# A two-layer hybrid block on one core: rotation tables from phases summed once for all groups, factors stored in three parts, scans woven two steps sooner

## The chip, the core and the metric

The kernel runs on one core of one Trainium2 chip. The metric is the device time of one execution in microseconds (us). Five engines work at once, each through its own list of instructions, in order: PE multiplies matrices (PEld is its weight load, which overlaps), DVE and ACT do element-wise work (ACT also table functions such as Sin, Silu and Gelu), POOL does a little of both, SP only issues DMAs. ACT and POOL issue DMAs too; the rows mark such issues with a q (SPq, ACTq, POOLq).

## What is computed

The reference runs two layers over 1024 latent tokens and 256 context tokens of width 1024. Layer 0 has gated linear recurrences. Layer 1, where the change lies, has windowed attention beside a bidirectional diagonal state-space model ("S5"): 64 groups of 16 channels, each with 64 complex states per direction. Cut to what matters:

```python
lam = lax.complex(lam_re[direction], lam_im[direction])
dt = jnp.exp(log_dt[direction])[:, None]
abar = jnp.exp(lam * dt)
bbar = ((abar - 1.0) / lam)[:, :, None] * bmat
st_c = diag_scan(abar, order(jnp.einsum('blgh,gph->lbgp', uc_cx, bbar)), None)
st_l = order(diag_scan(abar, order(jnp.einsum('blgh,gph->lbgp', ul_cx, bbar)), st_c[-1]))
y_l = y_l + read(st_l)        # real part of states times cmat
```

After it come a gelu, a gated linear unit (GLU) of width 2 x 1024 and the output projection.

## The kernel before, in words

Nearly all matmul work is `mm3` (lines 69 to 71): each fp32 product as three products of a high and a low part. A weight unit of 128x1024 arrives by a DMA from SP (`wraw`, L116) and is split into `whi` (ACT, L64) and `wlo` (DVE, L65).

**Layer 1** (`layer1`) weaves two generators. `main` has 88 steps, each one matmul group and its evacuation: 24 for u (S5's input, written to DRAM by L950), 10 for v, 6 for k and 48 for queries and gates; k and q go through `rope` (L895 on ACT, L897 to L899 on DVE, DMAs from ACT, L902 and L970). `side` is S5's `run`, then eight steps that read S5's output z back (`zr`, L941) and split it (`zh`, `zl`) for the GLU, whose matmuls need all of z. `weave(main, side, nm, ns)` takes a step of `side` whenever it is behind the ratio ns/nm of the steps of `main`. It fixes the order in which the program is written. The order on each engine is then laid out ahead of time by the framework's planner, from planned durations, with the earlier written instruction first where several are ready; so an engine's list does not follow the written order strictly, and once laid out it is kept.

**S5.** The states' powers are taken out of the scan: the drive is rotated by a table of cos and sin, scanned with a real decay, and rotated back. The work goes in 32 pairs of groups:
- `params` (L1290 on, once): step sizes, factors and powers for all 64 groups, on DVE, in a pool of its own ("s5t") that is given up after it. The factors lie in one tile `blk` of 128x16x512: columns 384 to 512 the powers (L1368 to L1371), 0 to 192 the outputs 0 to 2 (L1414 to L1420), 192 to 384 the outputs 3 to 5 (L1421 to L1428). One DMA of SP (L1429) writes it to DRAM when all is there. `build_a` reads 16 pieces of it back (`bq`, L1486).
- `table_a` (ACT, L1557 and L1558): r, the whole turns of n times the phase, for n = 0 to 159, of the two groups.
- `table_b` (DVE): n times the phase's high and low part, less r (L1567, L1568, each once per group), and what is left of whole turns (L1569, L1570).
- `table_c` (ACT): sin, absolute value, cos (L1579 to L1581) and the decay (`dec`, L1583).
- `front_a` (PE L1605, ACT L1609 to L1611): the drive `sd`. `front_b` (DVE L1622 to L1632): rotate, scan (L1626), rotate back into `uw`, which has two buffers; ACT copies it to `sx` (L1634, L1635). `back` (PE L1645 and L1647, ACT L1649; every fourth pair a Gelu, L1651, and DMAs of POOL, L1654).
- `build_a` and `build_b` make the matrices of four groups by turns (DVE L1545 to L1547, PE L1498 to L1521, DMAs L1526 and L1529).

After the weave `g_att` (attention) starts beside the GLU; its first loads (`kr`, L1103) go into memory that `main`'s operands held until then.

Of the kernel before, what the change touches and what calls it, by code (L numbers as in the profile page):

```python
# [9 lines left out]
F32 = mybir.dt.float32  # L10
# [3 lines left out]
AF = mybir.ActivationFunctionType  # L14
OP = mybir.AluOpType
# [39 lines left out]
class Body:  # L55
# [848 lines left out]
    def layer1(self):  # L904
# [23 lines left out]
        with tc.tile_pool(name="psum1", bufs=1, space=PSUM, reuse_waits="tile") as ps5:  # L928
            s5 = S5(self, ps5, uF, zF)
            nu = [0]  # L930
            zx = ExitStack()
            hz = []

            def side():
                yield from s5.run(nu)
                zp = zx.enter_context(tc.tile_pool(name="zt", bufs=1, reuse_waits="tile"))
                zh, zl = (zp.tile([128, 8, 1024], F32R, name=f"z{x}") for x in "hl")
                hz.extend([zh[:, :, c:c + 512], zl[:, :, c:c + 512], c, 512] for c in (0, 512))
                for cb in range(8):
                    t = zp.tile([128, 1024], F32, name="zr", tag="zr", bufs=2)  # L940
                    nc.sync.dma_start(t, zF[cb].rearrange("g h t n -> (g h) (t n)"))  # L941
                    self.split(zh[:, cb], zl[:, cb], t)
                    yield

            def main():
                for i in range(8):
                    def ev_u(ps, c0, n):
                        t = self.stg.tile([128, 512], F32, name="sg", tag="sg", bufs=2)[:, :n].rearrange("p (t n) -> p t n", t=8)
                        S.activation(t, ps.rearrange("p (n t) -> p t n", t=8), AF.Copy)
                        self.nc.scalar.dma_start(  # L950
                            uF[i * 8:i * 8 + 8, :, c0 // 8:(c0 + n) // 8].rearrange("g (h t) n -> (g h) t n", t=8), t)

                    yield from self.g_fm(st, self.hs, ev_u)
                    nu[0] += 1

                def ev_v(ps, b):
                    t = self.stg.tile([128, 512], F32, name="sg", tag="sg", bufs=2)[:, :256]
                    S.activation(t, ps, AF.Copy)
                    self.nc.scalar.dma_start(vD[b], t)

                yield from self.g_tm(st, self.hs, ev_v)
                for i in range(2):
                    def ev_k(ps, c0, n):
                        if c0:
                            self.rope(ps, c0, n, 1.0, [kD[i, o:o + 32, c0:c0 + n] for o in (0, 64, 32, 96)])
                            return
                        r = self.stg.tile([128, 512], F32, name="rp", tag="rp", bufs=3)
                        S.activation(r[:, :n], ps, AF.Copy)
                        for j, o in enumerate((0, 64, 32, 96)):
                            self.nc.scalar.dma_start(kD[i, o:o + 32, :n], r[j * 32:j * 32 + 32, :n])  # L970

                    yield from self.g_fm(st, self.hs, ev_k)
                self.h1c.close()
                for kind, i in oB:
                    def ev(ps, c0, n):
                        lc = slice(c0 - 256, c0 - 256 + n)
                        if kind == "q":
                            self.rope(ps, c0, n, 0.125, [
                                qD[lc.start // 128:lc.stop // 128, i // 2, a * 32:a * 32 + 32,
                                   i % 2 * 2 + h].rearrange("b d t -> d b t")  # L980
                                for a in range(2) for h in range(2)])
                        elif kind == "ga":
                            t = self.silu(ps, n)
                            self.nc.scalar.dma_start(gaD[i, :, lc], t)
                        else:
                            t = self.stg.tile([128, 8, 64], F32, name="sg", tag="sg", bufs=2)
                            S.activation(t, ps.rearrange("p (n t) -> p t n", t=8)[:, ::-1], AF.Silu)
                            self.nc.scalar.dma_start(gsD[i, :, :, lc.start // 8:lc.stop // 8], t)

                    yield from self.g_fm(st, self.hs[1:], ev)  # L990

            weave(main(), side(), 24 + 10 + 6 + 2 * len(oB) - 4, s5.steps + 9)
        self.right.close()
        if self.stop == "l1":
            self.show(qD, kD, vD, gaD, gsD, zF)
# [260 lines left out]
class S5:  # L1256
# [33 lines left out]
    def params(self):  # L1290
# [75 lines left out]
        for i in range(2):  # L1366
            q = pw[:, i].rearrange("p (c g) t -> p c g t", g=4)
            V.tensor_copy(pg[0:64, i], q[0:64, :, :, 7::-1])  # L1368
            V.tensor_copy(pg[64:128, i], q[64:128, :, :, 0:8])
            V.tensor_copy(pg[0:64, 2 + i], q[0:64, :, :, 8:0:-1])  # L1370
            V.tensor_copy(pg[64:128, 2 + i], q[64:128, :, :, 1:9])  # L1371
        yield

        ts(a, wr, 8.0, None, op0=OP.mult)
# [26 lines left out]
        tt(b, b, b, op=OP.mult)  # L1401
        ts(c8, b, -2.0, 1.0, op0=OP.mult, op1=OP.add)
        yield

        t1 = self.wt("s5t", (128, 16, 4, 16), 1)

# [3 lines left out]
        def out(i):  # L1410
            return blk[:, :, i * 64:i * 64 + 64].rearrange("p c (g h) -> p c g h", g=4)
# [6 lines left out]
        tt(t1, br, col(1), op=OP.mult)  # L1418
        stt(out(1), out(1), -1.0, t1, op0=OP.mult, op1=OP.subtract)
        ts(out(2), out(0), -1.0, None, op0=OP.mult)  # L1420
        tt(out(4), cr, col(5), op=OP.mult)  # L1421
        tt(t1, ci, col(6), op=OP.mult)
        tt(out(4), out(4), t1, op=OP.add)
# [2 lines left out]
        tt(t1, cr, col(6), op=OP.mult)  # L1426
        tt(out(5), out(5), t1, op=OP.subtract)
        ts(out(3), out(5), -1.0, None, op0=OP.mult)  # L1428
        self.nc.sync.dma_start(self.K.s5blk.rearrange("c p n -> p c n"), blk)  # L1429
        yield  # L1430

    def run(self, nu):
# [1 line left out]
        nc, left, tile_pool = self.nc, ExitStack(), self.K.tc.tile_pool  # L1434
        par = left.enter_context(tile_pool(name="s5p", bufs=1, reuse_waits="tile"))
        self.k5 = par.tile([128, 8, 64], F32, name="s5k5")
        self.nidx = par.tile([128, 322], F32, name="nidx")
        nc.sync.dma_start(self.nidx, self.A["nidx"])
        with tile_pool(name="s5t", bufs=1, reuse_waits="tile") as self.work:
            yield from self.params()  # L1440
# [10 lines left out]
        build()  # L1451
        yield
        build()
        self.table_a(0)
        self.table_b(0)
        self.table_c(0)
        yield
# [1 line left out]
        for p in range(32):  # L1459
            assert nu[0] * 4 > p  # L1460
            q = self.front_a(p)
            if p < 31:
                self.table_a(p + 1)
            yield
            self.front_b(q)
            if p < 31:
                self.table_b(p + 1)
            yield
            todo.append(q)
            if len(todo) > 2:  # L1470
                self.back(todo.pop(0))
            if p < 31:
                self.table_c(p + 1)
            build()
            yield
# [73 lines left out]
    def col(self, i, p, g):  # L1549
        return self.k5[:, i, p * 2 + g:p * 2 + g + 1]  # L1550

    def table_a(self, p):

        n, mag, nmag = (self.nidx[:, a:b] for a, b in ((0, 160), (320, 321), (321, 322)))
        r = self.wt("tb", (128, 2, 160), 2)
        for g in range(2):
            self.S.activation(r[:, g], n, AF.Identity, scale=self.col(7, p, g), bias=mag)  # L1557
        self.S.activation(r, r, AF.Identity, bias=nmag)  # L1558
        self.tabs[p] = r

    def table_b(self, p):

        V = self.V
        n, r = self.nidx[:, :160], self.tabs[p]
        u = self.wt("tb", (128, 2, 160), 2)
        for g in range(2):
            V.scalar_tensor_tensor(u[:, g], n, self.col(3, p, g), r[:, g], op0=OP.mult, op1=OP.subtract)  # L1567
            V.scalar_tensor_tensor(u[:, g], n, self.col(4, p, g), u[:, g], op0=OP.mult, op1=OP.add)  # L1568
        V.tensor_scalar(r, u, MAG, MAG, op0=OP.add, op1=OP.subtract)  # L1569
        V.tensor_tensor(u, u, r, op=OP.subtract)  # L1570
        self.tabs[p] = r, u

    def table_c(self, p):

        S = self.S
        w, u = self.tabs[p]
        tab = self.wt("tab", (128, 2, 2, 160), 2)
        dec = self.wt("dec", (128, 2, 2, 160), 2)
        S.activation(tab[:, :, 1], u, AF.Sin, scale=TURN)  # L1579
        S.activation(w, u, AF.Abs)  # L1580
        S.activation(tab[:, :, 0], w, AF.Sin, scale=-TURN, bias=self.K.halfpi)  # L1581
        for g in range(2):
            S.activation(dec[:, :, g], self.nidx[:, None, 160:320].to_broadcast([128, 2, 160]), AF.Copy,  # L1583
                         scale=self.col(2, p, g))
        self.tabs[p] = tab, dec

# [27 lines left out]
    def front_b(self, q):  # L1614
# [10 lines left out]
        Q = RQ[:, 0]  # L1625
        V.tensor_tensor_scan(*(x.rearrange("p a b n -> p (a b n)") for x in (Q, dec, D)), 0.0, op0=OP.mult, op1=OP.add)  # L1626
        sh = [128, 2, 2, 2, 128]
        UW = self.wt("uw", sh, 2)
        tt(UW, Q[:, :, :, None, 31:159].to_broadcast(sh), tab[:, None, :, :, 32:160].to_broadcast(sh), op=OP.mult)
        U, W = UW[:, 0], UW[:, 1]  # L1630
        tt(U[:, :, 0], U[:, :, 0], W[:, :, 1], op=OP.add)
# [54 lines left out]
def s5_host(f, A):  # L1686
# [15 lines left out]
    for h in range(16):  # L1702
        d[112 + h, :, h] = f["s5_d"][0][:, h]
    A["s5d"] = d
    A["nidx"] = np.broadcast_to(np.concatenate([np.arange(160), np.arange(160) > 0, [MAG, -MAG]]), (128, 322)).astype(np.float32)
    sh = np.zeros((128, 128), np.float32)
    sh[np.arange(16), np.arange(16) + 112] = 1
    A["shift"] = sh
# [88 lines left out]
```

## Time and profile before

| | |
|---|---|
| runs timed | 3: 2754.64, 2755.33, 2758.05 us |
| median | 2755.33 us |
| the profiled execution | 2752.66 us, span 2750.9 us |
| PE, DVE, ACT busy | 96%, 69%, 51% of the span |
| layer 1's weave and the start of the GLU | about 1565 to 2170 us of the span |

The busy times count what the profiler saw at work; PE's matmuls are pipelined, so its 96% is not a measure of how near it is to its peak. "PEclk" is the granted clock of the matrix engine as a share of 2.4 GHz; it has two levels, 1.2 and 2.4 GHz, and a stretch's number is their mean. A row of idle time names what ended most of it.

### The profile page before, as it was taken

The numbers are of one execution on the slowest core, as the hardware profiler recorded it, in microseconds if no ns is written. First come the engines' busy times: TensorE is split into PE (matmuls) and PEld (weight loads), VectorE is DVE, ScalarE is ACT, GpSimd is POOL, SyncE is SP. The second block draws the span as 40 slices with busy tenths as digits, with TensorE's granted clock in tenths as the row PEclk, the third lists the DMA queues.
The fourth block names the chain that finished last, engine by engine and source line by source line (L and its number), as shares of the span: only waits on it lengthen the run. The fifth ranks groups of instructions, "written<-read, shape, count | busy, mean of one in ns | idle before, by whom it ended". The sixth has DMA issues, their size and how long they took to land.

```text
span 2750.9 us, 44818 instructions
## 1 busy us (share of the span) xinstructions
PE 2648.8 (96%) x15680; PEld 2277.7 (83%) x15680; DVE 1890.4 (69%) x4884; ACT 1414.0 (51%) x3010; POOL 486.1 (18%) x881
## 2 busy tenths in 40 slices
PE   6999999999999999998999999899999899999998
PEld 3998989888898888887887788778888788887887
DVE  5556656554565546637457678899995888889886
ACT  5545545434445436437233316777776655556551
POOL 1021120212212222223000000010001112223430
PEclk9999999999999999999999999999999899999999
DMA  6101011111110111123464444344444623234253
GB/s 241 33 24 57 28 49 41 49 51 54 56 57 31 57 56 41 51 68 108 134 205 129 159 130 125 96 120 118 117 121 122 181 86 101 90 100 152 91 174 110
DMA packets 231394, 262.23 MB, mean 95 GB/s; under 512 B 87489, under 2 KB 173761, under 8 KB 230913
## 3 DMA queue, kind: packets, MB, share of 16 engines
q1 hardware_dynamic: 170400, 223.96, 26.6%
q10 hardware_dynamic: 55712, 20.46, 2.9%
q0 software_dynamic: 5056, 14.95, 1.8%
q8 instruction: 124, 2.03, 0.3%
q14 instruction: 102, 0.83, 0.1%
HBM read 192.76 MB, written 66.52 MB: 94 GB/s over the span
## 4 chain that ended last, share of the span: by engine, by line
PE 67%; DVE 16%; ACT 8%; DMA 5%; issue 3%; SPq 1%; ACTq 0%; POOL 0%; DVEq 0%
PE mm L69 17%; PE mm L70 16%; PE mm L71 16%; PE o L547 3%; PE st L558 2%; PE pt L1172 2%; PE att L518 2%; DVE tmp L448 2%; PE sc L1141 1%; ACT L399 1%; PE sc L1142 1%; PE pv L1181 1%; PE pv L1180 1%; PE att L519 1%; DVE rq L1626 1%
## 5 line engine op out<-in xcount | busy, mean ns | idle before, releaser
L69 PE MATMUL mm<-hh,whi 128*128 128x512 f32 (+1 forms) x1800 | 670.4, 373 | 14.9 <-ACT gt L583 5.1
L71 PE MATMUL mm<-hh,wlo 128*128 128x512 f32 (+1 forms) x1800 | 668.6, 372 | 0.4 <-DVE wlo L65 0.4
L70 PE MATMUL mm<-hl,whi 128*128 128x512 f32 (+1 forms) x1800 | 664.6, 369 | 0.5 <-DVE hl L65 0.5
L69 PEld LDWEIGHTS mm<-hh,whi 128*128 128x128 f32 x1800 | 341.1, 190 | 69.1 <-issue 6.4
L71 PEld LDWEIGHTS mm<-hh,wlo 128*128 128x128 f32 x1800 | 340.5, 189 | 54.2 <-issue 1.6
L70 PEld LDWEIGHTS mm<-hl,whi 128*128 128x128 f32 x1800 | 340.8, 189 | 53.3 <-DVE hl L65 1.2
L70 PE MATMUL mm<-owl,yh 128*128 128x512 f32 x576 | 227.0, 395 | 1.7 <-DVE owl L65 1.5
L69 PE MATMUL mm<-owh,yh 128*128 128x512 f32 x576 | 226.1, 393 | 0.8 <-ACT yh L64 0.8
L71 PE MATMUL mm<-owh,yl 128*128 128x512 f32 x576 | 226.3, 393 | 0.5 <-DVE yl L65 0.5
L65 DVE TENSOR_TENSOR wlo<-wraw,whi 128x1024 fp32r<-128x1024 f32 x117 | 145.7, 1245 | 99.7 <-ACT whi L64 99.5
L69 PE MATMUL mm<-whi,hh 128*128 128x256 f32 x720 | 206.0, 286 | 3.1 <-DVE v L364 3.1
L70 PE MATMUL mm<-wlo,hh 128*128 128x256 f32 x720 | 205.0, 285 | 0.0
L71 PE MATMUL mm<-whi,hl 128*128 128x256 f32 x720 | 202.5, 281 | 0.0
L64 ACT ACTIVATE whi<-wraw 128x1024 fp32r<-128x1024 f32 x117 | 123.7, 1057 | 124.3 <-PE mm L70 97.0
L563 DVE SCALAR_TENSOR_TENSOR S<-S,sc,st 128x128 f32<-128x128 f32 (+1 forms) x192 | 74.3, 387 | 161.6 <-PE st L558 161.2
L1155 ACT ACTIVATE P<-P,ast 128x640 f32<-128x640 f32 (+1 forms) x128 | 101.6, 795 | 95.0 <-DVE ast L1156 62.5
L64 ACT ACTIVATE yh<-yr 128x256 fp32r<-128x256 f32 x144 | 53.4, 410 | 168.6 <-PE mm L70 87.9
L69 PEld LDWEIGHTS mm<-whi,hh 128*128 128x128 f32 x720 | 135.6, 188 | 5.1 <-DVE v L364 4.0
L70 PEld LDWEIGHTS mm<-wlo,hh 128*128 128x128 f32 x720 | 136.0, 189 | 1.2
L71 PEld LDWEIGHTS mm<-whi,hl 128*128 128x128 f32 x720 | 135.6, 188 | 0.8 <-issue 0.2
L1161 POOL TENSOR_TENSOR P<-P,ast 128x640 f32<-128x640 f32 (+1 forms) x64 | 84.0, 1312 | 293.9 <-DVE ast L1159 181.7
L70 PEld LDWEIGHTS mm<-owl,yh 128*128 128x128 f32 x576 | 108.2, 188 | 27.2 <-DVE owl L65 5.2
(403 smaller groups left out, 6217.2 us busy)
## 6 DMA issues: line engine op xcount, KB each, us to landing
wraw<-in_w SPq DMA_DIRECT2D x117, 512.0 KB, 3.7
yr<-yT SPq DMA_DIRECT2D x144, 128.0 KB, 2.9
owr<-in_wo SPq DMA_DIRECT2D x62, 256.0 KB, 5.4
whi<-in_wada SPq DMA_DIRECT2D x24, 512.0 KB, 3.5
adaw<-in_adaw SPq DMA_DIRECT2D x16, 512.0 KB, 10.2
qr<-qD SPq DMA_DIRECT2D x64, 128.0 KB, 3.2
yT<-gt SPq DMA_DIRECT2D x28, 256.0 KB, 2.3
x1p<-xr SPq DMA_DIRECT2D x10, 512.0 KB, 3.7
```

The source lines that it names most:

```text
L64: self.S.activation(hi, src, AF.Copy)
L65: (eng or self.V).tensor_tensor(lo, src, hi.bitcast(F32), op=OP.subtract)
L69: T.matmul(ps, sh, mh, start=first, stop=False)
L70: T.matmul(ps, sh, ml, start=False, stop=False)
L71: T.matmul(ps, sl, mh, start=False, stop=last)
L448: V.tensor_tensor_scan(cs.rearrange("p a b -> p (a b)"), self.scmask, gp.rearrange("p a b -> p (a b)"), 0.0, op0=OP.mult, op1=OP.add)
L518: T.matmul(ps[:, d * 128:d * 128 + 128], k1[d][:, c:c + 128], q1[d][:, c:c + 128], start=True, stop=True)
L547: T.matmul(ps[:, :dv], l, r, start=j == 0, stop=j == len(mms) - 1)
L558: T.matmul(pst[:, :dv], ktT[:, d * 128:d * 128 + 128], v[b], start=True, stop=True)
L563: V.scalar_tensor_tensor(new, state[d], scal(d, b, 6, 7), pst[:, :dv], op0=OP.mult, op1=OP.add)
L1155: S.activation(p[:, j, :w], p[:, j, :w], AF.Exp, bias=nm[:, j:j + 1], accum_out=sm[:, j:j + 1])
L1161: G.tensor_tensor(p[:, 1, :w], p[:, 1, :w], es[:, 1:2].to_broadcast([128, w]), op=OP.mult)
```

## The change

Phases: a point n of the table is written as 16a + b. The phases of 16a (10 values) and of b (16 values), less whole turns, are made once for all 64 groups in `params` (tile `ph`, 128x64x26, by six DVE instructions). `table_a` goes; `table_b` adds the two lists (one instruction for both groups) and takes whole turns off as before. The factors go to DRAM by three DMAs, each where its columns are ready. `uw` has one buffer in place of two. In the weave nm is 82 in place of 84. The list `nidx` is shorter.

```diff
@@ layer1
-            weave(main(), side(), 24 + 10 + 6 + 2 * len(oB) - 4, s5.steps + 9)
+            weave(main(), side(), 24 + 10 + 6 + 2 * len(oB) - 6, s5.steps + 9)
@@ params, behind L1371
+        def put(a, b):
+            self.nc.sync.dma_start(self.K.s5blk.rearrange("c p n -> p c n")[:, :, a:b], blk[:, :, a:b])
+
+        put(384, 512)
         yield
@@ params, behind L1402
         yield
+        r, sh = self.wt("s5r", (128, 64, 26), 1), [128, 64, 26]
+        n26 = self.nidx[:, None, 160:].to_broadcast(sh)
+        def col26(x):
+            return x[:, :, None].to_broadcast(sh)
+        tt(r, n26, col26(pht), op=OP.mult)
+        ts(r, r, MAG, MAG, op0=OP.add, op1=OP.subtract)
+        tt(self.ph, n26, col26(phh), op=OP.mult)
+        tt(self.ph, self.ph, r, op=OP.subtract)
+        tt(r, n26, col26(phl), op=OP.mult)
+        tt(self.ph, self.ph, r, op=OP.add)
@@ params, outputs
         ts(out(2), out(0), -1.0, None, op0=OP.mult)
+        put(0, 192)
...
         ts(out(3), out(5), -1.0, None, op0=OP.mult)
-        self.nc.sync.dma_start(self.K.s5blk.rearrange("c p n -> p c n"), blk)
+        put(192, 384)
         yield
@@ run
-        self.nidx = par.tile([128, 322], F32, name="nidx")
+        self.nidx = par.tile([128, 186], F32, name="nidx")
+        self.ph = par.tile([128, 64, 26], F32, name="s5ph")
...
-        self.table_a(0)
         self.table_b(0)
...
-            if p < 31:
-                self.table_a(p + 1)
@@ table_b
-        n, r = self.nidx[:, :160], self.tabs[p]
-        u = self.wt("tb", (128, 2, 160), 2)
-        for g in range(2):
-            V.scalar_tensor_tensor(u[:, g], n, self.col(3, p, g), r[:, g], op0=OP.mult, op1=OP.subtract)
-            V.scalar_tensor_tensor(u[:, g], n, self.col(4, p, g), u[:, g], op0=OP.mult, op1=OP.add)
+        r, u = (self.wt("tb", (128, 2, 160), 2) for _ in range(2))
+        ph, sh = self.ph[:, p * 2:p * 2 + 2], [128, 2, 10, 16]
+        V.tensor_tensor(u.rearrange("p g (a b) -> p g a b", b=16), ph[:, :, 0:10, None].to_broadcast(sh),
+                        ph[:, :, None, 10:26].to_broadcast(sh), op=OP.add)
         V.tensor_scalar(r, u, MAG, MAG, op0=OP.add, op1=OP.subtract)
         V.tensor_tensor(u, u, r, op=OP.subtract)
@@ front_b
-        UW = self.wt("uw", sh, 2)
+        UW = self.wt("uw", sh, 1)
```

`table_a` is removed whole, and the host's list `nidx` follows.

## Rows read from the trace of the kernel before

**Rows 1.** The span and clock of the core, and the page's busy times.
```profile
core 0: 2750.9 us, clock 0.989
...
PE 2648.8 (96%) x15680; PEld 2277.7 (83%) x15680; DVE 1890.4 (69%) x4884; ACT 1414.0 (51%) x3010; POOL 486.1 (18%) x881
```

**Rows 2.** Stretches of S5 and the GLU's start: length, busy times, PEclk, DMA.
```profile
1650.00:1730.00 80.00, 78.23 (x590) 71.23 (x589) 65.05 (x101) 50.62 (x112) 0.00 (x0) 1.00 0.47 118
1730.00:1850.00 120.00, 104.79 (x597) 88.07 (x596) 113.85 (x168) 89.96 (x168) 12.60 (x24) 0.96 0.46 113
1850.00:2088.00 238.00, 237.02 (x1326) 198.76 (x1325) 221.62 (x342) 179.96 (x341) 16.73 (x32) 1.00 0.46 113
2088.00:2100.00 12.00, 9.61 (x45) 8.30 (x44) 4.83 (x10) 7.21 (x14) 0.00 (x0) 0.86 0.48 142
...
2132.00:2170.00 38.00, 29.47 (x112) 21.79 (x111) 27.24 (x73) 25.19 (x45) 2.52 (x3) 0.78 0.91 242
```

**Rows 3.** PE's waits from 1650 to 2170: us in total, times, longest.
```profile
PE yo L1647 <- ACT sx L1635: 9.5, 3, 8.1
...
PE mm L69 <- ACT zh L64: 2.9, 1, 2.9
...
PE pd L1605 <- DMA mt<-s5kd: 2.4, 1, 2.4
```

**Rows 4.** Timeline about the end of params, DVE, then ACT; idle before in brackets.
```profile
1630.55 1.23 DVE L65 TENSOR_TENSOR wlo<-wraw,whi 128x1024 fp32r<-128x1024 f32 x1 [2.72 <-ACT whi L64]
...
1639.36 0.69 DVE L1428 TENSOR_SCALAR s5blk<-s5blk 128x1024 f32<-128x1024 f32 x1
...
1655.11 0.94 ACT L1557 ACTIVATE tb<-nidx,s5k 128x160 f32<-128x160 f32 x2 [8.09 <-DMA s5blk<-s5blk]
```

**Rows 5.** DVE by form, 1655 to 2120: busy us, mean ns, idle before.
```profile
L1567 DVE SCALAR_TENSOR_TENSOR tb<-nidx,s5k,tb 128x160 f32<-128x160 f32 x64 | 21.8, 378 | 17.9 <-DMA dd<-in_s5d 12.5 <-ACT tb L1558 5.2
L1568 DVE SCALAR_TENSOR_TENSOR tb<-nidx,s5k,tb 128x160 f32<-128x160 f32 x64 | 21.8, 375 | 0.0
...
L1545 DVE TENSOR_TENSOR G<-bq 128x1024 f32<-128x1024 f32 x16 | 19.5, 1219 | 2.2 <-PE pd L1605 1.3 <-PE sk L1504 0.5 <-DMA bq<-s5blk 0.3
...
L1570 DVE TENSOR_TENSOR tb<-tb 128x320 f32<-128x320 f32 x32 | 15.5, 484 | 0.0
...
L1569 DVE TENSOR_SCALAR tb<-tb 128x320 f32<-128x320 f32 x32 | 10.2, 318 | 0.1
```

**Rows 6.** ACT by form, 1655 to 2120.
```profile
L1557 ACT ACTIVATE tb<-nidx,s5k 128x160 f32<-128x160 f32 x64 | 29.6, 510 | 8.1 <-DMA s5blk<-s5blk 8.1
...
L1558 ACT ACTIVATE tb<-tb,nidx 128x320 f32<-128x320 f32 x32 | 17.9, 559 | 0.5
```

**Rows 7.** The 32 scans: shortest, median, longest ns, first and last start.
```profile
L1626 DVE TENSOR_TENSOR_SCAN rq<-dec,sd x32: 1479/1484/1493, 1683.1 to 2108.7; 128x640 f32<-128x640 f32 x32
```

**Rows 8.** Timeline of the longest wait of PE, with DVE's uw and ACT's sx.
```profile
1739.87 0.42 DVE L1632 TENSOR_TENSOR uw<-uw 128x256 f32<-128x256 f32 x1
...
1743.78 0.63 ACT L1635 ACTIVATE sx<-uw 64x512 f32<-64x512 f32 x1
...
1746.59 1.22 DVE L1629 TENSOR_TENSOR uw<-rq,tab 128x1024 f32<-128x1024 f32 x1
```

**Rows 9.** Timeline of SP's issues about the end of main.
```profile
2118.19 0.33 SPq L1088 DMA_DIRECT2D am<-in_amask  x1
2133.77 0.51 SPq L1103 DMA_DIRECT2D kr<-kD  x1
...
2135.29 0.33 SPq L941 DMA_DIRECT2D zr<-zF  x1
```

**Rows 10.** DMA issues: KB each, median us from issue to landing.
```profile
s5blk<-s5blk SPq DMA_DIRECT2D x1, 4096.0 KB, 14.9
...
gaD<-sg ACTq DMA_DIRECT2D x16, 256.0 KB, 2.8
gsD<-sg ACTq DMA_DIRECT2D x16, 256.0 KB, 3.1
```

More of the change, by code (lines that the diff above doesn't have):

```diff
@@ L1550, in col @@
         return self.k5[:, i, p * 2 + g:p * 2 + g + 1]
-    def table_a(self, p):
-        n, mag, nmag = (self.nidx[:, a:b] for a, b in ((0, 160), (320, 321), (321, 322)))
-        r = self.wt("tb", (128, 2, 160), 2)
-        for g in range(2):
-            self.S.activation(r[:, g], n, AF.Identity, scale=self.col(7, p, g), bias=mag)
-        self.S.activation(r, r, AF.Identity, bias=nmag)
-        self.tabs[p] = r
     def table_b(self, p):
         V = self.V
-        n, r = self.nidx[:, :160], self.tabs[p]
-        u = self.wt("tb", (128, 2, 160), 2)
-        for g in range(2):
-            V.scalar_tensor_tensor(u[:, g], n, self.col(3, p, g), r[:, g], op0=OP.mult, op1=OP.subtract)
-            V.scalar_tensor_tensor(u[:, g], n, self.col(4, p, g), u[:, g], op0=OP.mult, op1=OP.add)
+        r, u = (self.wt("tb", (128, 2, 160), 2) for _ in range(2))
+        ph, sh = self.ph[:, p * 2:p * 2 + 2], [128, 2, 10, 16]
+        V.tensor_tensor(u.rearrange("p g (a b) -> p g a b", b=16), ph[:, :, 0:10, None].to_broadcast(sh),
+                        ph[:, :, None, 10:26].to_broadcast(sh), op=OP.add)
         V.tensor_scalar(r, u, MAG, MAG, op0=OP.add, op1=OP.subtract)
@@ L1582, in table_c @@
         for g in range(2):
-            S.activation(dec[:, :, g], self.nidx[:, None, 160:320].to_broadcast([128, 2, 160]), AF.Copy,
+            S.activation(dec[:, :, g], self.nidx[:, None, :160].to_broadcast([128, 2, 160]), AF.Copy,
                          scale=self.col(2, p, g))
@@ L1704, in s5_host @@
     A["s5d"] = d
-    A["nidx"] = np.broadcast_to(np.concatenate([np.arange(160), np.arange(160) > 0, [MAG, -MAG]]), (128, 322)).astype(np.float32)
+    A["nidx"] = np.broadcast_to(np.concatenate([np.arange(160) > 0, np.arange(10) * 16, np.arange(16)]), (128, 186)).astype(np.float32)
     sh = np.zeros((128, 128), np.float32)
```

## The prediction, made before the change was run

> **What bounds the kernel now.** The page comes first: PE is busy for 96% of the span, DVE 69%, ACT 51% [rows 1]. PE's matmuls are untouched by the change, so time can only come out of stretches in which PE is idle or its clock is low. The table by stretches shows where these are in the part that the change touches [rows 2]. From 1850 to 2088 PE is idle for 1 us of 238 at full clock: nothing is to be had there, however much DVE and ACT work goes. From 1730 to 1850 it is idle for 15.2 us of 120 (120 less 104.79), while DVE is busy for 113.85, or 95%: PE waits behind the S5 chain, and DVE is what that chain runs on. From 2132 to 2170, at the start of the GLU, it is idle for 8.5 of 38 us and its clock is 0.78, between its levels of 1.2 and 2.4 GHz. Two small ones remain: 1.8 us in 1650 to 1730, 2.4 us in 2088 to 2100.
>
> The list of PE's waits names the links [rows 3]: 9.5 us for `sx`, the end of the rotation (8.1 in one piece); 2.9 us for `zh`, the first split of z; 2.4 us for a DMA (`mt`). The rows of the scans give S5's pace: 32 from 1683.1 to 2108.7, so 13.7 us a pair [rows 7].
>
> **The change, part by part.**
>
> *Phases in params.* Six new DVE instructions over 64x26 = 1664 elements. A broadcast product of 1024 (L1545) takes 1219 ns and a sum of 320 (L1570) 484, so 1.04 ns an element and 1.89 us for 1664, five times; the one with two constants goes from 0.318 us (320) and 0.69 us (1024) to 1.03 us [rows 4, 5]. Together 10.5 us. DVE has a hole of 2.7 us at the right place; the other 7.8 us push the last factor (L1428) from 1640.05 to 1647.8 [rows 4]. That is hidden if the last DMA becomes shorter by as much, since S5's first instructions wait for it; without that cover it costs up to 7.8 us of S5's start, though not of PE's time, which has `main` to do.
>
> *Factors in three DMAs.* The one DMA of 4096 KB takes 14.9 us and starts when all is there [rows 10]. The last piece is 192 of 512 columns: 5.6 us in proportion. Its lines are 768 bytes, not 2 KB; no row has such a piece. The lower bound is 5.6. For the upper one, `gsD` (pieces of 256 bytes) against `gaD` (2 KB), both 256 KB, is 3.1 against 2.8 us, a factor of 1.11 [rows 10]; 5.6 times that, and all 2.8 us of a small DMA as fixed cost, is 9.0. I take 6.5, near the proportion, as most of the 14.9 us is bytes. So the data lands at 1654.3 where it landed at 1655.0; by the bounds 1653.4 to 1656.8. The start of S5 stays where it was. The two early pieces move 2.6 MB beside weight loads on the same SP queue, and SP holds what is behind them until DVE has the columns. I cost that at nothing, hidden by a weight unit loaded ahead; without it, once, the 5.6 us of a piece.
> The Trainium skill ("DMA: Bandwidth & Descriptors", rules for kernel authors) advises to coalesce small transfers into large ones, which speaks against the split, but calls small what is under 64 KB; at its line rate for 512 bytes and more the last piece would keep to the proportion, 5.6 us, and the sum would be the same.
>
> *ACT's hold.* ACT stood for 8.1 us at the first `table_a`, with `main`'s evacuations behind it [rows 4]. With `table_a` gone, `dec` or a drive copy is late next, for the same DMA, but the wait planned around it is shorter. PE lost at most 1.8 us there [rows 2]: I take 1 (bounds 0 and 1.8).
>
> *Tables, per pair.* DVE loses L1567 and L1568 (21.8 us each over the 32 pairs) and gains one sum of the form of L1570 (15.5 us for 32) [rows 5]: 28.1 us, or 0.88 a pair. Both operands are broadcast; the factor product L1545 is broadcast too and costs no more per element than L1570, so I price that at nothing. ACT loses 29.6 + 17.9 = 47.5 us, or 1.5 a pair [rows 6], and the chain one hop from ACT to DVE.
> The Trainium skill ("VectorE: DVE Perf Modes", the errata on a fixed latency per instruction) puts such an instruction at 58 cycles and one per element at 0.96 GHz: an estimate of 227 ns for 160 and 394 for 320, so 16.5 us saved in place of 28.1; by that the sum below would be 15 in place of 21. The same section says that this row of it reads low and gives 151 cycles for a tensor_tensor: 324 and 491 ns, 25.8 us. The rows read 376 and 484 ns, so the trace agrees with the second, and measurement decides.
>
> *What that is worth from 1730 to 1850.* 120 us hold 8.7 pairs, so 7.7 us of DVE work go where DVE is 95% busy. I take PE's idle time to shrink by that, to 7.5 us; next late are ACT's Gelu, `rope` and table loads. The clock of 0.96 is worth 4.8 us over the stretch; with half the idle time gone I add 1.3 for it. Together 9 us. Bounds: nothing, since lists are laid out anew, and 20 (15.2 + 4.8).
>
> *The start of the GLU.* Today the last scan starts at 2108.7 and `main` ends at 2133.8: 25 us, in which the last outputs have to be read out, written, loaded as `zr` and split. Only part fits. SP shows why: from 2118.5 it stands before `kr`, whose memory `main` holds to its end, and the third `zr` follows behind it at 2135.3 [rows 9]. With 28 us less on DVE the scans end some 25 us sooner (28.1 times DVE's share of 93% in 1850 to 2088 [rows 2]), while `main` ends as before: about 50 us, and the z steps are written before the attention's loads with two more steps of `main` after them. PE's loss here is 8.5 us idle, and 22% of the clock over 29.5 busy us, 6.5: together 15. I take 11, as attention's own start stays; bounds 3 and 15.
>
> *The weave's number.* By itself nothing. The last scan is written at side step 103 of 113, so at main step 77 of 88, 11 ahead of the end. The 88 steps fill some 569 us, 6.5 each, so its place is about 70 us ahead of the end; it runs 25 us ahead of it [rows 7, 9]. S5 is behind its written place throughout, so writing it earlier cannot make it start earlier; only the z steps move, and they are counted above.
>
> *`uw` with one buffer.* DVE's next `uw` must wait for ACT's two copies of the last. At the tightest place I found, the copies end at 1744.41 and the next `uw` starts at 1746.59 [rows 8]: 2.2 us of room, less 0.9 for the shorter pair. Cost nothing; if the cover goes, see the second rival.
>
> *The stop at 2088.* A wait for the `mt` DMA; I leave it, bounds plus and minus 2.4 [rows 2, 3].
>
> **Sum.** 1 + 9 + 11 = 21 us less. The profiled execution took 2752.66 us with a span of 2750.9 [rows 1], so 2731.7. It lies 2.7 us under the median of the runs, 2755.33; against that the forecast is 2734. Not all bounds come at once; half way to each side gives 2724 to 2747 for this case.
>
> **Rivals.**
> 1. *The holes only move* (no change, 2752 to 2760). The lists are laid out from planned durations; the 8.1 us piece is a place where PE's list put S5's product well before ACT had it. A new layout may put as many such places elsewhere. For it: PE's idle time is few long waits, not many short ones [rows 3]. Against: with DVE at 95% any delay persists, and the change takes off just that load.
> 2. *The single `uw` buffer makes DVE wait* (slower). Place: DVE, before L1629, every pair. From the end of L1632 (1740.29) to the end of L1635 (1744.41) was 4.1 us [rows 8]; the next pair's rotation and scan must fill it, in DVE's fixed order. It decides when the mean wait exceeds the 0.88 us saved per pair. With 2 us a pair, S5 ends 31 x 1.1 = 34 us later, past the 25 us that are left before `main` ends: PE waits some 9 us more there, and 8.7 pairs x 1.1 = 10 more in 1730 to 1850: about 2774. With half of that, about 2765.
> 3. *All of it comes back* (about 2716). Idle time in the four rows other than 1850 to 2088 is 27.9 us [rows 2], the clock of the two long ones another 11: 39 less, if the S5 chain is never late again.
> 4. *The weave does the work.* If S5 did follow its written place, two steps, 13 us, would be gained at the GLU alone, of which its 11 can be used, and the tables would be worth nothing: about 2744, inside the forecast.
>
> **How the numbers follow.** The forecast has 0.62 (rival 4 within it), all back 0.13, the holes move 0.14, slower 0.11. This kernel's measurement can tell about 0.2%, 5.5 us, from no change. Of the forecast's cases 0.02 end within that, so faster is 0.73, the same 0.16, slower 0.11. The range goes from 2718 (most of the way to rival 3) to 2757 (rival 1's middle); beyond are rival 2 and the ends of 1 and 3.
>
> **What would show it.** Right: no L1557; six DVE instructions of about 1.9 and 1.0 us in params; one of 0.48 us per pair in place of four; a last DMA of 5.6 to 9 us that lands near 1654; the last scan some 25 us before its old place; DVE under 90% and PE idle below 9 us in the stretch that was 1730 to 1850; clock 1.00 and idle time under 4 us at the GLU's start; all `zr` issued before `kr`. Wrong: a scan pace still near 13.7 us, DVE waiting for `sx` before L1629, or new PE waits of 5 us and more.

## The result, and the profile after

The kernel after takes 2723.24 us (median of 4 runs, 2719.62 to 2724.97) against 2754.98 before (a fourth run included): ratio 0.9881, 95% interval 0.9864 to 0.9898, so 32 us less where 21 were forecast. The profiled execution took 2724.01 us. Its span and busy times answer to [rows 1]; this is the view of the cores, then the page's first part.

```profile
core 0: 2722.2 us, clock 0.990
...
PE 2636.9 (97%) x15680; PEld 2274.3 (84%) x15680; DVE 1861.4 (68%) x4794; ACT 1374.3 (50%) x2917; POOL 488.4 (18%) x881
```

DVE lost 90 instructions (three of four in each of 32 pairs, less the six for the lists) and 29.0 us, ACT 93 by the records and 39.7 us. The span fell by 28.7 us. PE's idle time (span less busy) fell from 102.1 to 85.3, by 16.8; the other 11.9 is less busy time for the same 15680 matmuls. The table by stretches, columns as in [rows 2], says where:

```profile
1650.00:1730.00 80.00, 79.97 (x597) 72.97 (x596) 63.14 (x86) 44.33 (x94) 4.22 (x8) 1.00 0.49 126
1730.00:1850.00 120.00, 109.12 (x650) 92.71 (x650) 115.64 (x159) 87.14 (x163) 8.34 (x16) 0.96 0.43 110
1850.00:2088.00 238.00, 233.03 (x1301) 195.97 (x1300) 212.71 (x295) 168.08 (x300) 20.84 (x40) 0.99 0.50 126
2088.00:2100.00 12.00, 12.00 (x54) 9.80 (x53) 6.04 (x6) 5.67 (x7) 0.00 (x0) 1.00 0.94 287
...
2132.00:2170.00 38.00, 38.00 (x194) 32.33 (x193) 24.69 (x64) 19.81 (x37) 3.29 (x3) 1.00 0.72 191
```

The start of the GLU (last line) is mended: no idle time, clock 1.00, where there were 8.5 us and 0.78. The first stretch lost its 1.8 us. But 1730 to 1850 keeps 10.9 us of its 15.2, with DVE still at 96%, and 1850 to 2088, which had 1.0, now has 5.0. The list of PE's waits from 1540 to 2200 (total, times, longest) agrees with it: no wait for `zh` is left, and the one for `sx` is as long as in [rows 3].

```profile
PE yo L1653 <- ACT sx L1641: 9.8, 3, 8.5
...
PE mm L69 <- ACT whi L64: 1.8, 2, 1.6
```

The scans, against [rows 7]: 12.09 us a pair in place of 13.73, and the last one 50.8 us sooner.

```profile
L1632 DVE TENSOR_TENSOR_SCAN rq<-dec,sd x32: 1479/1484/1493, 1683.1 to 2057.9; 128x640 f32<-128x640 f32 x32
```

So the loads of z are all issued before the attention's begin. In the views of the tiles `zr` and `kr` of after, the figures behind the count are the shortest, median and longest issue in ns:

```profile
L941 SPq DMA_DIRECT2D zr<-zF x8: 319/320/326, 2076.3 to 2102.0; - x8
...
L1103 SPq DMA_DIRECT2D kr<-kD x6: 445/500/591, 2128.4 to 2151.8; - x6
```

and in the same view of before, where they ran on beyond `main`'s end:

```profile
L941 SPq DMA_DIRECT2D zr<-zF x8: 320/326/334, 2114.0 to 2159.9; - x8
```

Cut at the first matmul of the GLU (the view of the tile `mm` gives its start, 2133.8 before and 2128.4 after), the 28.7 us fall into 5.4 ahead of it and 23.1 between it and the last matmul of the output projection, with 0.2 left over by rounding and the very end.

### The profile page after: what moved, and what is told of

Its sections match the earlier page's. It is cut to its first block, busy times and chain, and to the rows that moved or that the text cites. A ratio compares the mean times of both kernels' runs of the same rounds, so it can differ in the third digit from the quotient of the medians.

```text
span 2722.2 us, 44690 instructions
## 1 busy us (share of the span) xinstructions
PE 2636.9 (97%) x15680; PEld 2274.3 (84%) x15680; DVE 1861.4 (68%) x4794; ACT 1374.3 (50%) x2917; POOL 488.4 (18%) x881
## 5 line engine op out<-in xcount | busy, mean ns | idle before, releaser
L69 PE MATMUL mm<-hh,whi 128*128 128x512 f32 (+1 forms) x1800 | 671.4, 373 | 15.3 <-ACT gt L583 5.1
L69 PEld LDWEIGHTS mm<-hh,whi 128*128 128x128 f32 x1800 | 340.9, 189 | 69.5 <-issue 6.6
L69 PE MATMUL mm<-owh,yh 128*128 128x512 f32 x576 | 226.8, 395 | 1.4 <-ACT yh L64 1.4
L69 PE MATMUL mm<-whi,hh 128*128 128x256 f32 x720 | 205.7, 286 | 3.1 <-DVE v L364 3.1
L69 PEld LDWEIGHTS mm<-whi,hh 128*128 128x128 f32 x720 | 135.6, 188 | 5.1 <-DVE v L364 4.1
L69 PEld LDWEIGHTS mm<-owh,yh 128*128 128x128 f32 x576 | 108.2, 188 | 26.2 <-ACT ot L870 3.4
## 6 DMA issues: line engine op xcount, KB each, us to landing
adaw<-in_adaw SPq DMA_DIRECT2D x16, 512.0 KB, 10.2
```

The lines of the kernel that those rows point to most:

```text
L69: T.matmul(ps, sh, mh, start=first, stop=False)
```

## The experiments

Twelve kernels, in three sets: which part of the change carries the gain (e1 to e4), which part of the tables' work (e5 to e7), and what the gain hangs on downstream (e8 to e12). Ratios are to the kernel before, on the same chip. From each trace: the start of the last scan, the first matmul of the GLU (`zh` at L69), the GLU's length (from that start to the start of the last such matmul), and the tail, from the first matmul of the GLU to the start of the last L69 matmul of the output projection. These four come from one profiled execution each, which lies up to 4.7 us off the median (e1's, the slowest of its runs). Attention shares PE with the GLU and runs on after it, so the tail is the number to compare.

| kernel | median us | ratio, 95% interval | last scan | GLU starts | GLU | tail |
|---|---|---|---|---|---|---|
| before | 2754.98 | | 2108.7 | 2133.8 | 320.9 | 606.1 |
| after | 2723.24 | 0.9881 [0.9864, 0.9898] | 2057.9 | 2128.4 | 284.5 | 583.0 |
| e1 before + tables | 2729.42 | 0.9905 [0.9891, 0.9919] | 2085.3 | 2125.1 | 293.4 | 596.4 |
| e2 before + weave 82 | 2757.20 | 1.0006 [0.9997, 1.0015] | 2115.9 | 2144.1 | 329.1 | 603.2 |
| e3 before + three DMAs | 2759.43 | 1.0009 [1.0000, 1.0018] | 2114.5 | 2141.3 | 321.1 | 606.8 |
| e4 after, weave 84 | 2732.06 | 0.9909 [0.9893, 0.9924] | 2066.4 | 2130.9 | 284.5 | 588.2 |
| e5 after + DVE's load | 2747.17 | 0.9967 [0.9954, 0.9979] | 2090.3 | 2141.1 | 284.5 | 592.4 |
| e6 after + ACT's load | 2728.56 | 0.9900 [0.9885, 0.9915] | 2068.3 | 2129.9 | 284.5 | 585.3 |
| e7 after + ACT's load and hop | 2747.96 | 0.9969 [0.9957, 0.9980] | 2079.0 | 2142.6 | 284.6 | 590.2 |
| e8 before, z by POOL | 2760.93 | 1.0016 [1.0007, 1.0024] | 2108.2 | 2135.7 | 326.3 | 608.8 |
| e9 after, `ut` by POOL | 2714.26 | 0.9854 [0.9840, 0.9869] | 2046.0 | 2109.0 | 284.5 | 593.2 |
| e10 after, `s5kd` by POOL | 2715.91 | 0.9859 [0.9843, 0.9876] | 2051.1 | 2113.0 | 284.5 | 591.5 |
| e11 after, weave 78 | 2721.79 | 0.9882 [0.9867, 0.9897] | 2060.8 | 2129.9 | 284.5 | 579.4 |
| e12 after, z behind `kr` | 2753.21 | 0.9985 [0.9975, 0.9995] | 2058.9 | 2140.9 | 317.5 | 601.4 |

Four medians lie 1 us or more above the nearest range that was expected for them: e3 by 4 us, e7 and e8 by 3, e12 by 1. e4 lies only in its third range, that of holes that move.

### The parts alone: e1 to e4

**e1**: before, with the lists, the new `table_b` and the single `uw` buffer (the lists and the single buffer weren't taken apart); one DMA and the weave's 84 stay.

```diff
+        tt(r, n26, col26(pht), op=OP.mult)
...
-        self.nc.sync.dma_start(self.K.s5blk.rearrange("c p n -> p c n"), blk)
+        put(0, 512)
...
-        self.table_a(0)
...
-        UW = self.wt("uw", sh, 2)
+        UW = self.wt("uw", sh, 1)
```

> The kernel before with the phase lists and the single uw buffer, but one DMA for the factors and the old weave number. If the tables carry the gain (less DVE and ACT work, so S5's scans end early and z is ready for the GLU): 2722 to 2732 us, scan pace near 12.1 us a pair, no PE wait for zh. If the weave number carries it: 2745 to 2757. If the holes only move from one laid-out order to the next: anywhere from 2725 to 2755, with no link to the scan pace.

**e2**: before, with the weave's number alone.

```diff
-            weave(main(), side(), 24 + 10 + 6 + 2 * len(oB) - 4, s5.steps + 9)
+            weave(main(), side(), 24 + 10 + 6 + 2 * len(oB) - 6, s5.steps + 9)
```

> The kernel before with nm of 82 in place of 84 and nothing else. If S5 is behind its written place all the time: 2750 to 2757 us and a scan pace still near 13.7 us. If the weave number carries the gain: 2722 to 2740, the last scan 10 us or more before its old place of 2108.7.

**e3**: before, with the three DMAs alone.

```diff
+        put(384, 512)
...
+        put(0, 192)
...
-        self.nc.sync.dma_start(self.K.s5blk.rearrange("c p n -> p c n"), blk)
+        put(192, 384)
```

> The kernel before with the factors stored in three parts and nothing else. S5 then starts some 7 us earlier, as no phase list delays the last part. If only S5's rate counts: 2748 to 2755 us, pace 13.7, the last scan 5 to 8 us earlier. If the start counts: 2735 to 2745.

**e4**: after, with the weave's number back at 84.

```diff
-            weave(main(), side(), 24 + 10 + 6 + 2 * len(oB) - 6, s5.steps + 9)
+            weave(main(), side(), 24 + 10 + 6 + 2 * len(oB) - 4, s5.steps + 9)
```

> The changed kernel with nm back at 84. If the weave number does nothing by itself: 2720 to 2728 us, pace near 12.1. If it carries the gain: 2740 to 2755. If the holes only move: up to 10 us to either side of 2723.

The tables carry the change: e1 has 0.9905 of the 0.9881. The weave's number and the three DMAs alone are worth nothing that can be told. In e3 S5 did start some 10 us sooner (first scan at 1673.3, not 1683.1) and still ended 5.8 us later: an earlier start is lost again. The scans of e1:

```profile
L1630 DVE TENSOR_TENSOR_SCAN rq<-dec,sd x32: 1477/1482/1492, 1687.8 to 2085.3; 128x640 f32<-128x640 f32 x32
```

That is 12.82 us a pair, 0.91 less than before; the forecast's work per pair was 0.88. The last scan comes 23.4 us sooner, forecast some 25. The start of the GLU moved by 8.7 us and the tail by 9.7; the forecast had 10 (hold and stretch) and 11.

The rest of the change comes out of the combination. With the tables and the three DMAs but 84 (e4) the time is e1's; 82 then takes another 8 to 9 us off, though alone (e2) it does nothing. All four runs of e4 (2729.57 to 2732.40) lie above all four of after.

### DVE's load, ACT's load, the hop: e5 to e7

**e5**: two more DVE instructions of 320 elements per pair, each the maximum of `u` and itself, which leaves `u` as it is: about the DVE time that the change saved.

```diff
@@ table_b, behind the sum
+        for _ in range(2):
+            V.tensor_tensor(u, u, u, op=OP.max)
```

> The changed kernel with two DVE instructions of 0.48 us more per pair (a maximum of u with itself, twice), so DVE's load is back to that of before, ACT's is not. If S5's rate hangs on DVE's load: pace 13 us a pair or more, 2735 to 2750 us. If it hung on the hop from ACT to DVE that has gone: pace 12.1 to 12.6 and 2721 to 2730.

**e6**: three more ACT instructions per pair of the removed ones' shapes, written into a part of `dec` that ACT itself overwrites afterwards; no other engine waits for them.

```diff
@@ table_c
+        for g in range(2):
+            S.activation(dec[:, 0, g], self.nidx[:, :160], AF.Identity, scale=self.col(7, p, g))
+        S.activation(dec[:, 0], dec[:, 0], AF.Copy)
```

> The changed kernel with ACT's three instructions of table_a put back as idle work ahead of dec, so ACT's load is that of before, with no DVE instruction behind them. If ACT's load counts: pace 12.8 or more, 2735 to 2750 us. If not: pace 12.1 to 12.4 and 2720 to 2729.

**e7**: three of the same shapes at the old places, on the tile `r` into which DVE then rounds. Their values aren't used, but DVE's rounding must wait for them, as L1567 did for `table_a`.

```diff
@@ run
+        self.table_a(0)
         self.table_b(0)
...
+            if p < 31:
+                self.table_a(p + 1)
...
@@ table_b
-        r, u = (self.wt("tb", (128, 2, 160), 2) for _ in range(2))
+        r, u = self.tabs[p], self.wt("tb", (128, 2, 160), 2)
```

> The changed kernel with table_a's three ACT instructions written where they were and onto the same buffer, so that DVE's rounding must wait for them as before; their values are overwritten. If the hop counts (17 us of DVE waits for ACT's tables have gone with the change): pace 12.6 to 13, 2730 to 2745 us. If only DVE's load counts: as the changed kernel, 2720 to 2727.

e5 puts 24 us back. Its load, DVE by form from 1655 to 2120:

```profile
L1576 DVE TENSOR_TENSOR tb<-tb 128x320 f32<-128x320 f32 x64 | 30.8, 482 | 0.4
```

So 0.96 us more a pair, and the pace goes from 12.09 to 13.13 us, by 1.04: DVE's work passes into S5's pace one to one. e6, with 1.2 us a pair on ACT (its rows read 23.8 and 14.8 us; the change took 1.5 off), costs 5 us and 0.42 of pace. e7 costs 25 us and 0.75 of pace: the same ACT work, but DVE behind it. DVE's load and ACT's hop each undo most of the gain when put back alone; ACT's load hardly counts. In the waits of DVE from 1680 to 2110 of before two rows are ACT's tables. The second is the hop itself, from `table_a` to `table_b`; the first is the cos of `table_c`, a link from ACT to DVE that the change keeps:

```profile
DVE rq L1622 <- ACT tab L1581: 12.2, 10, 2.5
...
DVE tb L1567 <- ACT tb L1558: 5.2, 6, 2.7
```

Together 17.4 us in which DVE stood for a table that ACT was late with. The view of after, to 2060, has neither; its largest is not of the tables:

```profile
DVE rp L897 <- ACT rp L895: 6.7, 4, 4.1
```

The table of stretches sums it up for DVE, from the first scan to the last, before:

```profile
1683.00:2108.70 425.70, 406.69 (x2397) 346.33 (x2396) 389.02 (x594) 315.04 (x605) 29.34 (x56) 0.98 0.44 110
```

and after:

```profile
1683.00:2057.90 374.90, 359.02 (x2199) 307.76 (x2198) 358.35 (x501) 270.51 (x510) 29.24 (x56) 0.98 0.46 113
```

DVE was busy for 30.7 us less and idle for 20.1 less (36.7 to 16.6): together the 50.8 by which the last scan moved.

One thing goes beyond the scans: e5 and e7 still have a GLU of 284.5 us, yet it starts 13 and 14 us late. Idle time from 1650 to the GLU's start is 23.7 and 26.3 us there, 15.9 after. So a slower S5 is paid in `main`, which waits for S5's products, even where z comes in time. Another 9.4 and 7.2 us of tail lie behind the GLU, where PE is idle for 16.0 and 15.0 us against 9.6 in after; that part is not explained.

### What the gain hangs on: e8 and e12

**e8**: before, with the loads of z issued by POOL, past SP's queue.

```diff
-                    nc.sync.dma_start(t, zF[cb].rearrange("g h t n -> (g h) (t n)"))
+                    nc.gpsimd.dma_start(t, zF[cb].rearrange("g h t n -> (g h) (t n)"))
```

> The kernel before with the eight loads of z issued from POOL's queue, not SP's, so that none stands behind kr. If the place in the queue made the GLU's start slow: 2742 to 2750 us, PE idle in 2132 to 2200 half of its 8.5 us. If z is late because the scans end late: 2752 to 2758.

**e12**: after, with z's loads and splits written in `g_glu` and each load ordered behind the first `kr` on SP; the scans stay as they are.

```diff
@@ side
-                    t = zp.tile([128, 1024], F32, name="zr", tag="zr", bufs=2)
-                    nc.sync.dma_start(t, zF[cb].rearrange("g h t n -> (g h) (t n)"))
-                    self.split(zh[:, cb], zl[:, cb], t)
                     yield
@@ g_glu, behind its first yield
+        self.zload()
```

> The changed kernel with one thing made as late as it was before: the eight loads of z are tied behind the attention's first kr load on SP's queue, so they start when main ends. S5 is as fast as in the changed kernel. If the gain lies at the GLU's start: 2738 to 2752 us, the GLU's matmuls spread over 300 us or more in place of 284.5, PE waiting for zh and zl. If the gain lies in S5's stretch: 2721 to 2730.

e8 gives nothing, rather a loss of 4 us. POOL began the loads at 2125.5, later than SP's 2114.0 in before, and took 0.53 us for each where SP took 0.32: another queue, with the scans as late as they were (2108.2), does not bring z in sooner. POOL first had the last writes of z itself to issue (2121.3 to 2125.5), and in four of the six later loads it stood for the split of an earlier one, 16.1 us together. e12 is the counterpart, with early scans and late z. The tile views of its scans and of `zr`:

```profile
L1642 DVE TENSOR_TENSOR_SCAN rq<-dec,sd x32: 1482/1484/1492, 1683.8 to 2058.9; 128x640 f32<-128x640 f32 x32
```

```profile
L943 SPq DMA_DIRECT2D zr<-zF x8: 325/364/530, 2134.8 to 2167.2; - x8
```

and its stretch around the GLU's start:

```profile
2133.00:2200.00 67.00, 55.03 (x271) 45.88 (x272) 54.09 (x140) 40.35 (x78) 10.37 (x9) 0.85 0.68 186
```

12 us idle, a clock of 0.85, and of the gain 0.15% of the time is left: the span is 30.9 us longer than after's, 12.5 of it ahead of the first `zh` matmul and 18.4 in the tail. The longest wait goes from `main`'s end, some 3 us ahead of this stretch, to the attention's first matmul, and the first split of z (`zh`) started only at 2139.8, behind it:

```profile
2139.33 0.58 PE L1151 MATMUL sc<-kh,qa 128*128 128x256 f32 x1 [9.67 <-DVE qa L1129]
```

But e12 makes z later than it was before: its first load is issued at 2134.8, behind the attention's first eight loads, where before had issued two from 2114.0 on, and its GLU starts 7 us later than before's. So its 30.9 us may well be more than the old order would have cost; how much more no run shows. Early scans are worth next to nothing where z comes this late; and by e5 and e7 early z with a GLU at full clock is worth only some 8 us against before where S5 is slow. The full gain needs both. (In e12 the splits moved with the loads; their part in the 30.9 us was not taken apart.)

### The hole that stayed: e9 to e11

The 8.1 us wait of [rows 3], whose place is in [rows 8], came back as 8.5, at the same place. PE in the timeline of after, idle before in brackets:

```profile
1744.63 1.22 PE L1653 MATMUL yo<-sx,ct 128*128 128x128 f32 x4 [8.53 <-ACT sx L1641]
```

Between the fourth and fifth scan lie 28 us (1709.9 to 1738.3) at a pace of 12. SP's timeline (start, length, and how many issues in a row):

```profile
1705.71 8.39 SPq L1542 DMA_DIRECT2D s5kd<-kfb  x15
1714.27 4.70 SPq L1545 DMA_DIRECT2D mt<-s5kd  x8
1719.02 3.70 SPq L1604 DMA_DIRECT2D ut<-uF  x8
```

SP issues without a pause for 17 us, and `ut`, which the next pair's drive needs, stands at the end. The theory: SP's issue time and order make the hole. The rival: S5's own chain does.

**e9** and **e10**: after, with `ut` or `s5kd` issued by POOL.

```diff
-                nc.sync.dma_start(self.ut[t * 16:t * 16 + 16],
+                nc.gpsimd.dma_start(self.ut[t * 16:t * 16 + 16],
```

> The changed kernel with the 128 loads of S5's input pieces (ut) issued from POOL's queue, which is idle there, not from SP's. The one hole left in S5's stretch, 8.5 us near 1735, follows a gap of 28 us between the fourth and the fifth scan, while SP works through 15 small writes before it comes to these loads. If SP's order makes the gap: scans end 10 us or more earlier, idle of PE up to the GLU's start 16 to below 10, 2712 to 2719 us. If it is the wait for a free buffer: 2721 to 2728.

```diff
-                nc.sync.dma_start(kd[:, :, d * 7 + t].rearrange("g h o -> h g o"), kf[t * 16:t * 16 + 16, d])
+                nc.gpsimd.dma_start(kd[:, :, d * 7 + t].rearrange("g h o -> h g o"), kf[t * 16:t * 16 + 16, d])
```

> The changed kernel with the 240 small writes of the convolution matrices (s5kd) issued from POOL's queue. Takes 6.5 us per four groups off SP. If SP's order makes the gap: 2712 to 2719 us. If POOL's slower issue makes the matrices late: 2725 to 2740. If neither counts: 2720 to 2727.

**e11**: after, with the weave four main steps sooner still.

```diff
-            weave(main(), side(), 24 + 10 + 6 + 2 * len(oB) - 6, s5.steps + 9)
+            weave(main(), side(), 24 + 10 + 6 + 2 * len(oB) - 10, s5.steps + 9)
```

> The changed kernel with nm of 78 in place of 82. z is ready before the GLU already, so by the theory that only this counts nothing is left to gain there: 2719 to 2727 us. If writing S5 earlier by itself frees PE's list of holes (as 84 to 82 seemed to, 9 us): 2710 to 2718. If it pushes main's splits back: 2728 to 2740.

Both moves beat both kernels, by 7 to 9 us against after; e9 is the best version of the study, 2714.26 us. Its stretches:

```profile
1650.00:2109.00 459.00, 456.04 (x2718) 391.59 (x2717) 401.95 (x546) 309.52 (x570) 98.25 (x192) 1.00 0.50 131
...
1730.00:1850.00 120.00, 119.75 (x717) 102.11 (x716) 118.93 (x167) 89.92 (x169) 30.18 (x60) 1.00 0.48 118
```

PE is idle for 3 us from 1650 to the GLU's start, in place of 16, and 0.25 in the stretch that had 10.9, while DVE is at 99% there; the fifth scan follows the fourth after 9.7 us. So DVE's load was not what kept the last 8.5 us: SP's issues kept it. After's own trace agrees: between the end of the fourth scan and the start of the fifth DVE was idle for 10.6 of 27.0 us. The GLU starts 19.4 us sooner, but the tail is 10.2 us longer, so about half is given back in the attention; why was not tried. e11 gives nothing more.

## Why the prediction was right, and where its sizes were off

**The mechanism held**: tables faster, scans end sooner, z in before `main` ends, GLU starts without idle time at full clock. e1, e5, e7 and e12 each break or make one link of it. "By itself nothing" for the weave's number (e2) and nothing for the three DMAs (e3) stood too, and so rival 4 falls: the weave does not do the work. For rival 2 there is no sign: after's waits of DVE show none for `sx` at `uw` (e5's show one, of 1.8 us). Of rival 1 one piece came true: the one long hole stayed where it was, and 1850 to 2088 took 4 us back. The result lies between the forecast and rival 3; e9 reaches rival 3's 2716.

**Prices of instructions** were right. The sum of two lists, DVE by form in after, and two of the six instructions in `params`, from its timeline:

```profile
L1573 DVE TENSOR_TENSOR tb<-s5ph 128x320 f32<-128x320 f32 x32 | 15.5, 485 | 7.1 <-DMA s5blk<-s5blk 7.1
```

```profile
1628.71 1.88 DVE L1417 TENSOR_TENSOR s5ph<-nidx,s5k 128x1664 f32<-128x1664 f32 x1
...
1633.69 1.02 DVE L1416 TENSOR_SCALAR s5r<-s5r 128x1664 f32<-128x1664 f32 x1
...
1649.93 0.69 DVE L1446 TENSOR_SCALAR s5blk<-s5blk 128x1024 f32<-128x1024 f32 x1
```

The last of these rows is a factor, for the next point. 15.5 us for 32, as priced; the six together 10.44 us, forecast 10.5. Broadcasting both operands costs nothing that shows. By the Trainium skill ("VectorE: DVE Perf Modes", the errata) 151 cycles and one per element at 0.96 GHz are an estimate of 491 ns for 320 and 1.89 us for 1664; the trace agrees (485, and 1.88 to 1.89), and not with that section's row of 58 cycles.

**The last DMA** landed outside its bounds. Issued at 1650.65, because the last factor was ready at 1650.6 and not at 1647.8 (two splits of weights and 1.2 us of idle time lie in between), it took 7.0 us where I took 6.5 (bounds 5.6 and 9.0); from the list of issues (KB each, median us to landing):

```profile
s5blk<-s5blk SPq DMA_DIRECT2D x2, 1536.0 KB, 6.8
s5blk<-s5blk SPq DMA_DIRECT2D x1, 1024.0 KB, 5.2
```

It landed at about 1657.7, beyond the upper bound of 1656.8 and 2.7 us after its old time. The proportion to [rows 10] gives 5.6 and 3.7 us for the two sizes; 1.2 and 1.5 more were paid (the last section has a reading of it). It cost PE nothing: ACT's hold (before `dec`) shrank from 8.09 us to 3.34 and the stretch 1650 to 1730 lost all its idle time, near the upper bound of 1.8 where I took 1.

```profile
1657.69 1.92 ACT L1589 ACTIVATE dec<-nidx,s5k 128x320 f32<-128x320 f32 x4 [3.34 <-DMA s5blk<-s5blk]
```

**1730 to 1850**: forecast 9, got 4.3 of idle time and nothing of the clock, and 4.0 were given back in 1850 to 2088. The step that failed is that PE's idle time shrinks by DVE's saving because DVE is at 95%. 8.5 of the 10.9 us that stayed are one hole, which by e9 and e10 is SP's. A share of 95% over a stretch did not say what ended the one long wait in it. My test for this step (DVE under 90%, idle below 9) failed both ways.

**The scans**: some 25 us forecast, 50.8 measured. I counted DVE's work (28.1 us, measured 30.7) and named the hop from ACT, but gave DVE's idle time no price, and it fell by 20.1 us. That is the mis-sized term. The 17.4 us for ACT's tables could be read in DVE's waits, though only 5.2 of them are the hop; the 12.2 for the cos went too. With the hop put back (e7) DVE is idle for 37.0 us again, against 16.6, but not in one row: 2.5 us at the hop, 4.6 where `u` waits for ACT to have read its buffer, 7.6 for `sd`. Nor does the gain come by itself: in e1, where the two rows are gone as well, the time from the first scan to the last fell by only 28.1 us, because DVE waited elsewhere instead: its idle time there is 32.8 us, near before's 36.7. The longest of these waits is for a weight split of `main` that stood in DVE's list ahead of the last two scans:

```profile
2074.39 1.23 DVE L65 TENSOR_TENSOR wlo<-wraw,whi 128x1024 fp32r<-128x1024 f32 x1 [12.06 <-ACT whi L64]
```

Before had one of 7.1 us at the same place; in e4 and after such a wait (12.4 and 11.8 us) comes only behind the last scan. Then follow 4.7 us for PE's `yo` and 3.9 for the load of `bq`. The rest came with the other edits: the three DMAs brought the last scan 18.9 us forward from e1 to e4 (4.7 of it at the first scan), the weave's number 8.5 more. Why these edits lay the lists out so much better with the tables than without them stays open.

**The weave's number** on top of the tables is the other thing that I priced at nothing and that had a price. A reading that fits e4, after and e11: by my estimate of 6.5 us a step the last scan's written place, with 84, is 70 us ahead of `main`'s end, so at 2061 in e4, where it ran at 2066.4. S5 had caught up with its place there, and "S5 is behind its written place throughout" no longer held. With 82 the place is near 2044 and the scan ran at 2057.9; with 78 (e11) nothing more comes. The wait of 12.06 us in e1, also with 84, would be of that kind, as S5 waits there for `main`'s work; e4 has none ahead of its last scan. It was not tried further.

**The start of the GLU**: forecast 11 (bounds 3 and 15), and the tail shrank by 23.1. Before, from the first `zh` matmul:

```profile
2133.80:2170.00 36.20, 27.67 (x104) 20.33 (x103) 27.20 (x72) 25.19 (x45) 2.52 (x3) 0.76 0.96 254
```

8.5 us idle and 24% of 27.67 at the clock, 6.6: all 15.1 came. I had held 4 back for the attention's own start, which claimed none of it. Of the other 8, 3.3 are less idle time behind the GLU (12.9 to 9.6 us); 4.7 I cannot place.

**Sum**: on the profiled executions 28.7 us less where 21 were forecast, 5.4 for 10 ahead of the GLU and 23.1 for 11 behind it. These are two errors of opposite sign, so that the sum came as near as it did is in part luck. The medians lie 31.7 apart, as the execution profiled before was 2.3 us under its median and the one after 0.8 over. What stays open is why 82 after 84 with the tables (e4) takes 2.5 us off ahead of the GLU and 5.2 behind it, with the GLU at 284.5 us in both; each edit lays the lists out anew, and holes of this size in the attention come and go with it.

## What to carry to other kernels

For a serial chain on one engine, price two things: the work it does per step, and what it waits for on other engines per step; the second is in its waits even when it is small each time. Ask of each gain upstream which deadline downstream it meets: here 15.1 of the 28.7 us came at the start of the GLU, where eight loads got in ahead of the attention's. And before a hole is put down to the busiest engine, read the queue that issues the DMAs into it.

## What the runs showed of the hardware that was not expected

- SP's issue time is a resource. 31 issues in a row (15, 8 and 8) took 16.8 us, 0.54 each. Moving 128 of them to POOL, which takes 0.51 us for each and was nearly idle, gave 7 to 9 us with the same bytes moved. The Trainium skill ("Trainium Kernel Development and Optimization", Key Constraints) says that issuing from several engines only saves the sequencer's issue time; e9 agrees, and shows that here the hole on PE hung on this time.
- A DMA from on-chip memory cut by columns does not keep to the proportion of its bytes: 4096 KB took 14.9 us [rows 10], 1536 KB 6.8 to 7.0 and 1024 KB 5.2. The three lie on one straight line: an estimate of 2.0 us for any size and 3.2 us for each 1024 KB gives 14.8, 6.8 and 5.2, although their pieces are of 2 KB, 768 and 512 bytes. So a fixed part accounts for what was paid above the proportion, and the length of the pieces need not.
